# A Winograd-like left half in the second MLP product: seven block products, weight sums made by adding transfers, chunks interleaved

## Chip, cores and metric

One Trainium2 chip, one core. The time is the device time of one execution in microseconds (us). The kernel is a float32 decoder trunk of two layers whose weights (about 480 MB) are read once from device memory.

## The reference

For 256 tokens of width 2048, layer 0 mixes tokens with a Mamba-2 SSD mixer and layer 1 with a dilated sliding-window attention; each layer is followed by a squared-ReLU MLP, and a final RMSNorm closes the trunk. What the change touches is the MLP:

```python
def sq_relu_mlp(h, w1, w2):          # h (256, 2048), w1 (2048, 8192), w2 (8192, 2048)
    a = jax.nn.relu(h @ w1)
    return (a * a) @ w2
...
        x = x + sq_relu_mlp(rms_norm(x, norm_mlp[i]), mlp_w1[i], mlp_w2[i])
    return rms_norm(x, final_norm)
```

## The kernel before, in words

Every large product is made in a split form. A float32 weight block of 128x2048 (1 MB) is fetched from memory into a buffer `raw` (L141). ScalarE (ACT) copies it into `wh`, which rounds it to the type that TensorE (PE) multiplies at full rate (L142), and VectorE (DVE) subtracts to get the rest, `wl` (L143). The left operand is held in the same two parts, and three products stand for one: high by high, high by low, low by high. One such block is called a unit. `unit_plan` lists all units in the order in which PE uses them; `take` hands out the next one and fetches units up to three ahead (`LOOKAHEAD`), with three buffers each of `raw`, `wh` and `wl`.

The MLP goes through the 8192 hidden columns in 8 chunks of 1024. For a chunk, eight w1 units (called U here) make 128 hidden columns each, transposed, in one PSUM bank (`cols_units`, matmuls L169, tile `h`). Each is evacuated on ACT and DVE: the two bank halves are added (L187, L189), ReLU and the token's norm factor are applied (L721), the square is taken (L722) and the result is split into the two parts of `act` (L723, L724). Then eight w2 units (called D) multiply `act` by w2: unit (j, q) is rows 512q to 512q+511 of the chunk by output columns 512j to 512j+511, for both halves of the tokens (`rows_unit`, L203 to L205, tile `d`: 2 x 4 x 3 = 24 matmuls). After both q of a j, `add_residual` adds two banks into the running sum `x_res` (L210). The eight U of the next chunk come before the eight D of this one.

The instructions of an engine are put in order by the scheduler of the framework, from priorities and a timeline that it computes itself; `tc.issue_after` pins an instruction behind another one of the same engine. Loads go out on SP's queue. GpSimd (POOL) makes a few small operations. At the very end (`gained`, and the loop behind `mlp(1, ...)`) the squares of `x_res` are summed, `x_res` is multiplied by the final gain into `xf` (L766), and after the mean is known (L775, L777) `xf` is scaled (L781, L783) and stored.

Of the kernel before, what the change touches and what calls it, by code (L numbers as in the profile page):

```python
# [8 lines left out]
F32 = mybir.dt.float32  # L9
# [5 lines left out]
P = 128  # L15
# [22 lines left out]
FC = 8  # L38
# [25 lines left out]
    return plan  # L64


def mlp_plan(layer):
    plan = [("w1", layer, 0, u) for u in range(8)]
    for c in range(FC):
        if c + 1 < FC:  # L70
            plan += [("w1", layer, c + 1, u) for u in range(8)]
        plan += [("w2", layer, c, j, q) for j in range(4) for q in range(2)]
    return plan


# [1 line left out]
def hybrid_trunk_kernel(ctx: ExitStack, tc: tile.TileContext, a: dict, out: bass.AP):  # L77
# [8 lines left out]
    def mm_bank(name):  # L86
        return psum.tile([P, 512], F32, tag="mm", name=name, bufs=4)
# [19 lines left out]

    warm(2)
    plan = unit_plan()
    ready, load, high = {}, {}, {}  # L110
    cursor = [0, 0]
    latest = [None]

    def source(u):
        kind = u[0]
        if kind == "in":
            return a["w_in"][u[1] * 10 + u[2]], 2048
        if kind == "dt":
            return a["w_dt"], 2048
        if kind == "out":  # L120
            return a["w_out"][u[1] * 4 + u[2]], 2048
        if kind == "qk":
# [7 lines left out]
        return a["w2"][((u[1] * FC + u[2]) * 4 + u[3]) * 2 + u[4]], 2048  # L130

    def fetch(i, ends=(16,)):

        src, n = source(plan[i])
        raw = wts.tile([P, 2048], F32, tag="raw", name=f"raw{i}", bufs=3)
# [42 lines left out]
    def cols_many(us, xs, names, cuts=(12,)):  # L178

        banks = cols_units(us[:2], xs, names[:2], cuts, first=True)  # L180
        yield from banks
        for u, name in zip(us[2:], names[2:]):
            yield cols_units([u], xs, [name])[0]

    def cols_sum(ps, name):
        cross = work.tile([P, S], F32, tag="cross", name=name + "x", bufs=2)
        nc.scalar.activation(cross, ps[:, S:], AF.Copy)  # L187
        tot = work.tile([P, S], F32, tag="tot", name=name + "t", bufs=2)
        nc.vector.tensor_tensor(tot, ps[:, :S], cross, ALU.add)  # L189
        return tot  # L190

    def rows_unit(banks, us, lhs, k0, nk, n, first, last):

        ws = [take(*u) for u in us]
        kn = nk * len(us)
        for m in range(NH):
            t = slice(m * P, (m + 1) * P)
            for i in range(kn):
                wh, wl = ws[i // nk]
                c = slice((i % nk) * n, (i % nk + 1) * n)  # L200
                st, sp = first and i == 0, last and i == kn - 1
# [3 lines left out]
                nc.tensor.matmul(banks[m][:, :n], lo, wh[:, c], start=False, stop=sp)  # L205
# [498 lines left out]


    def mlp(layer, pool, xn, done):
        xs, rs, rb = xn.xs, xn.rs, xn.rb

        def up(c):
            act = pool.tile([P, 8, 2, S], F32R, tag="act", name=f"act{layer}_{c}", bufs=2)  # L710
            us, names = [("w1", layer, c, u) for u in range(8)], [f"h{layer}_{c}_{u}" for u in range(8)]
            if c == 0:
                made = cols_many(us, xs, names)
            else:
                made = (cols_units([u], xs, [name], first=name == names[0])[0]
                        for u, name in zip(us, names))
            for u, ps in enumerate(made):
                name = names[u]
                tot = cols_sum(ps, name)
                r = pool.tile([P, S], F32, tag="r", name=name + "r", bufs=2)  # L720
                nc.vector.scalar_tensor_tensor(r, tot, 0.0, rb, op0=ALU.max, op1=ALU.mult)  # L721
                nc.scalar.activation(r, r, AF.Square)  # L722
                nc.scalar.activation(act[:, u, 0, :], r, AF.Copy)  # L723
                nc.vector.tensor_tensor(act[:, u, 1, :], r, act[:, u, 0, :].bitcast(F32), ALU.subtract)  # L724
            return act

        def down(c, act):
            lhs = lambda k, part, t: act[:, k, part, t]
            for j in range(4):
                banks = [mm_bank(f"d{layer}_{c}_{j}_{m}") for m in range(NH)]  # L730
                us = [("w2", layer, c, j, q) for q in range(2)]
                if c == FC - 1 and j == 3:
                    rows_unit(banks, us, lhs, 0, 4, 512, True, True)
                else:
                    for q in range(2):
                        rows_unit(banks, us[q:q + 1], lhs, 4 * q, 4, 512, q == 0, q == 1)
                add_residual(banks, j)
                if c == FC - 1:
                    done(j)

        cur = up(0)
        for c in range(FC):
            nxt = up(c + 1) if c + 1 < FC else None
            down(c, cur)
            cur = nxt

    n1, n2, n3 = Normed(1), Normed(2), Normed(3)
    with ExitStack() as ctx_ssm:
# [3 lines left out]
    with ExitStack() as ctx_att:  # L752
        attention(n2, n3)
    with tc.tile_pool(name="mlp1", bufs=1) as pool:
        fin = pool.tile([P, D], F32, name="fin")
        nc.scalar.dma_start(fin, a["final_norm"].to_broadcast([P, D]))
        ssq = pool.tile([P, NH, 4], F32, name="fssq")
        mean = pool.tile([P, NH, 28], F32, name="fmean")[:, :, :2]
        xf = pool.tile([P, NH, D], F32, name="xf")

        def gained(j):
            c = slice(j * 512, (j + 1) * 512)
            for m in range(NH):
                nc.scalar.activation(ssq_junk, x_res[:, m, c], AF.Square, accum_out=ssq[:, m, j:j + 1])
                eng = nc.vector if j == 3 else nc.gpsimd
                eng.tensor_tensor(xf[:, m, c], x_res[:, m, c], fin[:, c], ALU.mult)  # L766
# [110 lines left out]
```

## Time and profile before

| | |
|---|---|
| median of 3 runs | 2635.85 us (2635.45 to 2635.88) |
| profiled execution, its own time | 2636.67 us |
| span of the profiled execution | 2634.6 us |
| PE matmul busy | 2620.2 us (99%), 14145 matmuls |
| DVE busy | 1701.5 us (65%) |
| ACT busy | 1344.5 us (51%) |
| POOL busy | 109.7 us (4%) |
| moved by DMA | 489.82 MB, mean 186 GB/s |

The span runs from the first to the last instruction; the execution's own time includes what lies around it. Busy times are merged per engine, so overlapped instructions count once. A matmul's own duration is modelled and overlaps that of its neighbours; the distance between two starts says what it costs.

### The profile page before, as it was taken

To read this page: it belongs to the slowest core of one execution; us is meant where nothing else is said; L and a number is where in the kernel's file an instruction comes from. 1 tells how busy PE (TensorE), PEld (TensorE's weight loads), DVE (VectorE), ACT (ScalarE), POOL (GpSimd) and SP (SyncE) were. 2 spreads that over 40 slices of the span, in tenths; PEclk is the share of its full clock that TensorE was granted. 3 is DMA by queue.
4 is the path that set the end of the run, shared out by engine and by line. 5 is a ranking of instruction groups with operands and counts; after the bars stand their busy time and mean duration, and the time that the engine had idled before them with its cause. 6 is when DMAs were issued, how large, how long until landed. Compare 5 with 4: busy or idle time off the path is not lost.

```text
span 2634.6 us, 34347 instructions
## 1 busy us (share of the span) xinstructions
PE 2620.2 (99%) x14145; PEld 2243.9 (85%) x14145; DVE 1701.5 (65%) x1986; ACT 1344.5 (51%) x1676; POOL 109.7 (4%) x75
## 2 busy tenths in 40 slices
PE   9999999999999999999999999999999999999998
PEld 7888888888888888888888998988888888888887
DVE  7888687786655555555556666676665555555554
ACT  6676455554554444444446656656454444444443
POOL 0121021211000000000000000000000000000001
PEclk9999999999999999999999999999999999999999
DMA  7555555555555555555555454444455555555553
GB/s 282 204 176 192 192 192 178 190 181 187 178 190 192 192 192 192 192 191 188 190 188 181 174 170 163 156 158 157 158 208 192 192 192 192 192 191 192 191 188 133
DMA packets 73036, 489.82 MB, mean 186 GB/s; under 512 B 8112, under 2 KB 8752, under 8 KB 18864
## 3 DMA queue, kind: packets, MB, share of 16 engines
q1 hardware_dynamic: 70272, 477.54, 52.3%
q10 hardware_dynamic: 2608, 10.09, 1.2%
q8 instruction: 111, 1.82, 0.3%
q14 instruction: 45, 0.37, 0.0%
HBM read 485.44 MB, written 2.16 MB: 185 GB/s over the span
## 4 chain that ended last, share of the span: by engine, by line
PE 95%; DVE 2%; ACT 1%; DMA 1%; POOL 1%; issue 1%; SPq 0%; ACTq 0%; POOLq 0%; DVEq 0%
PE h L169 27%; PE qk L169 10%; PE d L203 9%; PE d L204 9%; PE d L205 9%; PE c L169 8%; PE wo L204 2%; PE wo L203 2%; PE wo L205 2%; PE z L204 2%; PE z L205 2%; PE z L203 2%; PE v L203 2%; PE v L204 2%; PE v L205 2%; DVE wl L143 1%
## 5 line engine op out<-in xcount | busy, mean ns | idle before, releaser
L143 DVE TENSOR_TENSOR wl<-raw,wh 128x2048 fp32r<-128x2048 f32 (+4 forms) x470 | 1031.1, 2195 | 805.4 <-ACT wh L142 804.7
L142 ACT ACTIVATE wh<-raw 128x2048 fp32r<-128x2048 f32 (+4 forms) x470 | 863.1, 1838 | 941.1 <-PE d L205 391.7
L169 PE MATMUL h<-xn,wh 128*128 128x512 f32 x2048 | 713.7, 394 | 0.0
L169 PE MATMUL h<-xn,wl 128*128 128x256 f32 x2048 | 571.2, 281 | 0.0
L169 PEld LDWEIGHTS h<-xn,wh 128*128 128x128 f32 x2048 | 384.0, 188 | 87.2
L205 PE MATMUL d<-wh,act 128*128 128x512 f32 x1024 | 398.6, 389 | 0.0
L203 PE MATMUL d<-wh,act 128*128 128x512 f32 x1024 | 398.5, 389 | 0.0
L204 PE MATMUL d<-wl,act 128*128 128x512 f32 x1024 | 398.2, 389 | 0.0
L169 PEld LDWEIGHTS h<-xn,wl 128*128 128x128 f32 x2048 | 383.5, 187 | 2.4 <-DVE wl L143 0.3
L169 PE MATMUL c<-xn,wh 128*128 128x512 f32 x768 | 272.9, 398 | 2.0 <-ACT wh L142 1.8
L169 PE MATMUL qk<-xn,wh 128*128 128x512 f32 x768 | 271.1, 395 | 0.0
L205 PEld LDWEIGHTS d<-wh,act 128*128 128x128 f32 x1024 | 192.2, 188 | 40.1
L203 PEld LDWEIGHTS d<-wh,act 128*128 128x128 f32 x1024 | 192.3, 188 | 39.8
L204 PEld LDWEIGHTS d<-wl,act 128*128 128x128 f32 x1024 | 192.2, 188 | 39.3
L169 PE MATMUL qk<-xn,wl 128*128 128x256 f32 x768 | 216.7, 284 | 0.0
L169 PE MATMUL c<-xn,wl 128*128 128x256 f32 x768 | 215.0, 282 | 0.8 <-DVE wl L143 0.8
L169 PEld LDWEIGHTS c<-xn,wh 128*128 128x128 f32 x768 | 143.9, 188 | 37.0 <-ACT wh L142 3.9
L169 PEld LDWEIGHTS qk<-xn,wh 128*128 128x128 f32 x768 | 144.0, 188 | 30.2
L169 PEld LDWEIGHTS c<-xn,wl 128*128 128x128 f32 x768 | 143.9, 188 | 3.3 <-DVE wl L143 1.1
L169 PEld LDWEIGHTS qk<-xn,wl 128*128 128x128 f32 x768 | 143.7, 188 | 3.2 <-issue 2.7
L210 DVE TENSOR_TENSOR x_res<-d,x_res 128x512 f32<-128x512 f32 x128 | 87.9, 687 | 36.7 <-PE d L205 36.7
L204 PE MATMUL z<-wl,xn 128*128 128x512 f32 x256 | 101.4, 396 | 0.5 <-DVE wl L143 0.5
(336 smaller groups left out, 2976.3 us busy)
## 6 DMA issues: line engine op xcount, KB each, us to landing
raw<-in_w SPq DMA_DIRECT2D x256, 1024.0 KB, 4.9
raw<-in_w_in SPq DMA_DIRECT2D x74, 1024.0 KB, 4.9
raw<-in_w_qk SPq DMA_DIRECT2D x48, 1024.0 KB, 4.9
raw<-in_w_out SPq DMA_DIRECT2D x32, 1024.0 KB, 4.9
raw<-in_w_v SPq DMA_DIRECT2D x32, 768.0 KB, 4.3
ab<-acs_rows ACTq DMA_DIRECT2D x8, 1024.0 KB, 6.1
raw<-in_w_o SPq DMA_DIRECT2D x8, 1024.0 KB, 4.8
raw<-in_w_in SPq DMA_DIRECT2D x6, 512.0 KB, 8.0
```

The costliest lines, as they stand in the source:

```text
L142: high[i] = nc.scalar.activation(wh[:, c], raw[:, c], AF.Copy).ins
L143: nc.vector.tensor_tensor(wl[:, c], raw[:, c], wh[:, c].bitcast(F32), ALU.subtract)
L169: latest[0] = nc.tensor.matmul(ps[:, :n], (wh, wl)[part][:, kt * P:(kt + 1) * P], xs[:, kt, :, :].rearrange("p a t -> p (a t)")[:, :n], st ...
L203: nc.tensor.matmul(banks[m][:, :n], hi, wh[:, c], start=st, stop=False)
L204: nc.tensor.matmul(banks[m][:, :n], hi, wl[:, c], start=False, stop=False)
L205: nc.tensor.matmul(banks[m][:, :n], lo, wh[:, c], start=False, stop=sp)
L210: nc.vector.tensor_tensor(xc, banks[m], xc, ALU.add)
```

## The change

The left half of a chunk's second product (output columns 0 to 1023) is a 2x2 by 2x2 block product: token halves by hidden halves, and hidden halves by output halves. For the first seven chunks of each layer it is now formed from seven block products P1 to P7 instead of eight, with sums of blocks as operands. A product is 12 matmuls for one weight block of 128x2048.

The sums of `act` blocks are formed by DVE from the unsplit squares, which are now kept in one tile `r` of 128x8x256, and are split into two parts each (`combine`). The sums of w2 blocks are formed in the tiles `wa` and `wb`: the first block is loaded from SP's queue, the further ones are added to it in place by transfers issued from GpSimd with an adding operation, each after the split of the sum before it. P4 takes the negated sum, which the split makes with a factor of -1. The seven products share three PSUM banks (`x`: P1, P6, P7, P4 in turn; `w`: P5, P3; `z`: P2), and after each the bank's running sum is added to or subtracted from one block of `x_res` (`put`).

The right half keeps its four D units. All PE work of a chunk, with the eight U of the next chunk, follows the list `CHUNK_ORDER`; the splits of MLP weights are pinned in the order of the plan. The last chunk of each layer stays as it was. In the tail the final gain is multiplied in place into `x_res`, and its load is issued when the last chunk's first column block is done, into the place of `wb`.

```diff
+CHUNK_ORDER = ("U0 U1 P1 U2 P2 U3 U4 P5 D20 D21 P3 U5 U6 P6 U7 D30 P7 D31 P4").split()
+WINOGRAD = {
+    "P1": ("wa", 0, 0, True), "P2": ("raw", 1, 0, True), "P5": ("wa", 0, 1, False),
+    "P3": ("wb", 1, 1, True), "P6": ("wa", 1, 1, False), "P7": ("wb", 0, 1, False),
+    "P4": ("wa", 1, 0, False),
+}
...
         for k0, k1 in zip((0, *ends), ends):
             c = slice(k0 * n // 16, k1 * n // 16)
-            load[i] = nc.sync.dma_start(raw[:, c], src[:, c]).ins
-            high[i] = nc.scalar.activation(wh[:, c], raw[:, c], AF.Copy).ins
-            nc.vector.tensor_tensor(wl[:, c], raw[:, c], wh[:, c].bitcast(F32), ALU.subtract)
+            if begins:
+                load[i] = nc.sync.dma_start(raw[:, c], src[:, c]).ins
+            else:
+                nc.gpsimd.dma_start(raw[:, c], src[:, c], accum_op=ALU.add)
+            with ExitStack() as order:
+                if plan[i][0] in ("w1", "w2"):
+                    order.enter_context(tc.issue_after(high[i - 1]))
+                    order.enter_context(tc.issue_after(low[i - 1]))
+                if product == "P4":
+                    high[i] = nc.scalar.activation(wh[:, c], raw[:, c], AF.Copy, scale=-1.0).ins
+                    low[i] = nc.vector.scalar_tensor_tensor(
+                        wl[:, c], raw[:, c], -1.0, wh[:, c].bitcast(F32),
+                        op0=ALU.mult, op1=ALU.subtract).ins
...
+        def combine(c, r):
+            t1, t2 = slice(0, P), slice(P, S)
+            a11, a12, a21, a22 = r[:, :4, t1], r[:, 4:, t1], r[:, :4, t2], r[:, 4:, t2]
...
+            nc.vector.tensor_tensor(s[0], a21, a22, ALU.subtract)
+            split(1, s[0])
+            nc.vector.scalar_tensor_tensor(s[1], s[0], -1.0, a11, op0=ALU.mult, op1=ALU.subtract)
+            split(2, s[1])
+            nc.vector.scalar_tensor_tensor(s4, a12, -1.0, s[1], op0=ALU.mult, op1=ALU.subtract)
+            split(4, s4)
+            nc.vector.tensor_tensor(s3, a11, a21, ALU.add)
+            split(3, s3)
...
+        def product(c, item, ps, lhs, first):
+            wh, wl = take("w2", layer, c, item)
+            with tc.issue_after(latest[0]):
+                for i in range(4):
+                    n = slice(i * 512, (i + 1) * 512)
+                    for part, w in ((0, wh), (0, wl), (1, wh)):
+                        latest[0] = nc.tensor.matmul(
+                            ps, lhs(i, part), w[:, n], start=(first and i == 0 and part == 0 and w is wh),
+                            stop=(i == 3 and part == 1), skip_group_check=True).ins
+        def put(m, j, ps, op):
+            xc = x_res[:, m, j * 512:(j + 1) * 512]
+            nc.vector.tensor_tensor(xc, xc, ps, op)
...
+                    for m, j, op in {"P1": [(0, 0, ALU.add)], "P2": [(0, 0, ALU.add)],
+                                     "P5": [(1, 1, ALU.add)], "P3": [(0, 1, ALU.subtract)],
+                                     "P6": [(0, 1, ALU.subtract)], "P7": [(1, 1, ALU.add)],
+                                     "P4": [(1, 0, ALU.subtract)]}[item]:
+                        put(m, j, banks[where], op)
...
-        xf = pool.tile([P, NH, D], F32, name="xf")
+        xf = x_res
         def gained(j):
+            if j == 0:
+                fin.append(pool.tile([P, D], F32, tag="wb", name="fin", bufs=1))
+                nc.scalar.dma_start(fin[0], a["final_norm"].to_broadcast([P, D]))
```

## Rows read from the trace of the kernel before

**Rows 1.** The page: span, busy time by engine, the chain by engine.
```profile
span 2634.6 us, 34347 instructions
...
PE 2620.2 (99%) x14145; PEld 2243.9 (85%) x14145; DVE 1701.5 (65%) x1986; ACT 1344.5 (51%) x1676; POOL 109.7 (4%) x75
...
PE 95%; DVE 2%; ACT 1%; DMA 1%; POOL 1%; issue 1%; SPq 0%; ACTq 0%; POOLq 0%; DVEq 0%
```
**Rows 2.** Windows, one MLP chunk: busy us by engine, PEclk, DMA share, GB/s.
```profile
2141.80:2230.00 88.20, 88.20 (x451) 75.16 (x450) 49.95 (x48) 38.61 (x40) 0.00 (x0) 1.00 0.55 191
```
**Rows 3.** The chain in order of time: start us, us, what.
```profile
2141.80 44.65 PE h L169 x256
2230.00 44.65 PE h L169 x256
```
**Rows 4.** Timeline of PE, one w2 unit: start us, us, instruction.
```profile
900.29 0.39 PE L203 MATMUL d<-wh,act 128*128 128x512 f32 x1
...
905.73 0.39 PE L203 MATMUL d<-wh,act 128*128 128x512 f32 x1
```
**Rows 5.** All waits of PE, whole run: us in total, times, longest.
```profile
PE c L169 <- ACT wh L142: 1.8, 2, 1.5
PE warm L106 <- DVE ssq_junk L101: 1.5, 1, 1.5
PE c L169 <- DVE wl L143: 0.8, 1, 0.8
PE yT L557 <- ACT xd L547: 0.7, 1, 0.7
PE z L204 <- DVE wl L143: 0.5, 1, 0.5
PE o L203 <- ACT oT L690: 0.5, 1, 0.5
```
**Rows 6.** Groups by line and shape: busy us, mean ns, idle before, releaser.
```profile
L143 DVE TENSOR_TENSOR wl<-raw,wh 128x2048 fp32r<-128x2048 f32 x419 | 959.9, 2291 | 742.5 <-ACT wh L142 741.8
L142 ACT ACTIVATE wh<-raw 128x2048 fp32r<-128x2048 f32 x419 | 802.3, 1915 | 908.0 <-PE d L205 391.7 <-PE h L169 309.5 <-PE wo L205 81.6
...
L210 DVE TENSOR_TENSOR x_res<-d,x_res 128x512 f32<-128x512 f32 x128 | 87.9, 687 | 36.7 <-PE d L205 36.7
...
L226 ACT ACTIVATE ssq_junk<-x_res 128x512 f32<-128x512 f32 x24 | 15.0, 625 | 9.5 <-DVE x_res L210 7.8 <-DVE xn L221 1.6
...
L414 DVE TENSOR_TENSOR xdds<-xdd,xdds 128x512 fp32r<-128x512 f32 x8 | 5.5, 682 | 0.0
```
**Rows 7.** Timeline of ACT, then DVE, at a chunk's start.
```profile
2230.04 1.92 ACT L142 ACTIVATE wh<-raw 128x2048 fp32r<-128x2048 f32 x1 [3.52 <-PE d L205]
...
2231.99 2.29 DVE L143 TENSOR_TENSOR wl<-raw,wh 128x2048 fp32r<-128x2048 f32 x1 [1.26 <-ACT wh L142]
2237.45 2.29 DVE L143 TENSOR_TENSOR wl<-raw,wh 128x2048 fp32r<-128x2048 f32 x1 [3.16 <-ACT wh L142]
2239.66 0.42 DVE L189 TENSOR_TENSOR h_0t<-h,h_0x 128x256 f32<-128x256 f32 x1
```
**Rows 8.** DMA issues: queue, count, KB each, median us to landing.
```profile
raw<-in_w SPq DMA_DIRECT2D x256, 1024.0 KB, 4.9
...
x_res<-in_x SPq DMA_DIRECT2D x2, 1024.0 KB, 8.0
...
fin<-in_final_norm ACTq DMA_DIRECT2D x1, 1024.0 KB, 6.5
```
**Rows 9.** Timeline of DVE, then ACT, in the tail.
```profile
2626.36 0.69 DVE L210 TENSOR_TENSOR x_res<-d,x_res 128x512 f32<-128x512 f32 x1 [1.68 <-PE d L205]
2627.08 0.69 DVE L766 TENSOR_TENSOR xf<-x_res,fin 128x512 f32<-128x512 f32 x1
2627.90 0.21 DVE L775 TENSOR_SCALAR fmean<-fssq,fmean 128x1 f32<-128x1 f32 x1
...
2627.14 0.63 ACT L764 ACTIVATE ssq_junk<-x_res 128x512 f32<-128x512 f32 x1 [2.01 <-DVE x_res L210]
```

More of the change, by code (lines that the diff above doesn't have):

```diff
@@ L70, in mlp_plan @@
         if c + 1 < FC:
-            plan += [("w1", layer, c + 1, u) for u in range(8)]
-        plan += [("w2", layer, c, j, q) for j in range(4) for q in range(2)]
+            for item in CHUNK_ORDER:
+                if item[0] == "U":
+                    plan.append(("w1", layer, c + 1, int(item[1])))
+                elif item[0] == "P":
+                    plan.append(("w2", layer, c, item))
+                else:
+                    plan.append(("w2", layer, c, int(item[1]), int(item[2])))
+        else:
+            plan += [("w2", layer, c, j, q) for j in range(4) for q in range(2)]
     return plan
@@ L109, in hybrid_trunk_kernel @@
     plan = unit_plan()
-    ready, load, high = {}, {}, {}
+    ready, load, high, low = {}, {}, {}, {}
+    mlp_pool, sums_of = [None], {}
     cursor = [0, 0]
@@ L129, in source @@
             return a["w1"][(u[1] * FC + u[2]) * 8 + u[3]], 2048
-        return a["w2"][((u[1] * FC + u[2]) * 4 + u[3]) * 2 + u[4]], 2048
+        if len(u) == 4:
+            q, j = WINOGRAD[u[3]][1:3]
+        else:
+            j, q = u[3:]
+        return a["w2"][((u[1] * FC + u[2]) * 4 + j) * 2 + q], 2048
     def fetch(i, ends=(16,)):
         src, n = source(plan[i])
-        raw = wts.tile([P, 2048], F32, tag="raw", name=f"raw{i}", bufs=3)
+        product = plan[i][3] if plan[i][0] == "w2" and len(plan[i]) == 4 else None
+        where, _, _, begins = WINOGRAD.get(product, ("raw", 0, 0, True))
+        if where == "raw":
+            raw = wts.tile([P, 2048], F32, tag="raw", name=f"raw{i}", bufs=3)
+        elif begins:
+            raw = sums_of[where] = mlp_pool[0].tile([P, 2048], F32, tag=where, name=f"{where}{i}", bufs=1)
+        else:
+            raw = sums_of[where]
         wh = wts.tile([P, 2048], F32R, tag="wh", name=f"wh{i}", bufs=3)
@@ L140, in fetch @@
             c = slice(k0 * n // 16, k1 * n // 16)
-            load[i] = nc.sync.dma_start(raw[:, c], src[:, c]).ins
-            high[i] = nc.scalar.activation(wh[:, c], raw[:, c], AF.Copy).ins
-            nc.vector.tensor_tensor(wl[:, c], raw[:, c], wh[:, c].bitcast(F32), ALU.subtract)
+            if begins:
+                load[i] = nc.sync.dma_start(raw[:, c], src[:, c]).ins
+            else:
+                nc.gpsimd.dma_start(raw[:, c], src[:, c], accum_op=ALU.add)
[8 more added lines that the diff above has]
+                        op0=ALU.mult, op1=ALU.subtract).ins
+                else:
+                    high[i] = nc.scalar.activation(wh[:, c], raw[:, c], AF.Copy).ins
+                    low[i] = nc.vector.tensor_tensor(wl[:, c], raw[:, c], wh[:, c].bitcast(F32),
+                                                     ALU.subtract).ins
             yield
@@ L204, in rows_unit @@
                 nc.tensor.matmul(banks[m][:, :n], hi, wl[:, c], start=False, stop=False)
-                nc.tensor.matmul(banks[m][:, :n], lo, wh[:, c], start=False, stop=sp)
+                latest[0] = nc.tensor.matmul(banks[m][:, :n], lo, wh[:, c], start=False, stop=sp).ins
     def add_residual(banks, j):
@@ L727, in down @@
[L727 to L745, printed above, removed]
+        mlp_pool[0] = pool
+        def in_order(make):
+            with tc.issue_after(latest[0]):
+                return make()
+        def chunk(c):
+            act = pool.tile([P, 8, 2, S], F32R, tag="act", name=f"act{layer}_{c}", bufs=2)
+            r = pool.tile([P, 8, S], F32, tag="r", name=f"r{layer}_{c}", bufs=1)
+            return act, r
@@ new lines, in put, with half @@
+        def put(m, j, ps, op):
+            xc = x_res[:, m, j * 512:(j + 1) * 512]
+            nc.vector.tensor_tensor(xc, xc, ps, op)
+        act, r = chunk(0)
+        us, names = [("w1", layer, 0, u) for u in range(8)], [f"h{layer}_0_{u}" for u in range(8)]
+        for u, ps in enumerate(cols_many(us, xs, names)):
+            evacuate(0, u, ps, act, r)
+        for c in range(FC - 1):
+            parts = combine(c, r)
+            act_next, r_next = chunk(c + 1)
+            banks = {}
+            def half(k0, t):
+                return lambda i, part: act[:, k0 + i, part, t]
+            t1, t2 = slice(0, P), slice(P, S)
+            of = {"P1": half(0, t1), "P2": half(4, t1), "P4": half(4, t2)}
+            for k, item in ((1, "P5"), (2, "P6"), (3, "P7"), (4, "P3")):
+                of[item] = lambda i, part, k=k: parts[k][:, i, part]
+            lhs = lambda k, part, t: act[:, k, part, t]
+            for item in CHUNK_ORDER:
+                if item[0] == "U":
+                    u = int(item[1])
+                    ps = in_order(lambda: cols_units([("w1", layer, c + 1, u)], xs,
+                                                     [f"h{layer}_{c + 1}_{u}"], first=(u == 0))[0])
+                    evacuate(c + 1, u, ps, act_next, r_next)
+                elif item[0] == "D":
+                    j, q = int(item[1]), int(item[2])
+                    if q == 0:
+                        banks[j] = [mm_bank(f"d{layer}_{c}_{j}_{m}") for m in range(NH)]
+                    in_order(lambda: rows_unit(banks[j], [("w2", layer, c, j, q)], lhs, 4 * q, 4, 512,
+                                               q == 0, q == 1))
+                    if q == 1:
+                        add_residual(banks[j], j)
+                else:
+                    where = {"P1": "x", "P6": "x", "P7": "x", "P4": "x", "P5": "w", "P3": "w",
+                             "P2": "z"}[item]
+                    first = where not in banks
+                    if first:
+                        banks[where] = sm_bank(f"p{where}{layer}_{c}")
+                    product(c, item, banks[where], of[item], first)
+                    for m, j, op in {"P1": [(0, 0, ALU.add)], "P2": [(0, 0, ALU.add)],
[3 more added lines that the diff above has]
+                        put(m, j, banks[where], op)
+            act, r = act_next, r_next
@@ new lines, in mlp @@
+        c = FC - 1
+        lhs = lambda k, part, t: act[:, k, part, t]
+        for j in range(4):
+            banks = [mm_bank(f"d{layer}_{c}_{j}_{m}") for m in range(NH)]
+            us = [("w2", layer, c, j, q) for q in range(2)]
+            if j == 3:
+                rows_unit(banks, us, lhs, 0, 4, 512, True, True)
+            else:
+                for q in range(2):
+                    rows_unit(banks, us[q:q + 1], lhs, 4 * q, 4, 512, q == 0, q == 1)
+            add_residual(banks, j)
+            done(j)
@@ L765, in gained @@
                 eng = nc.vector if j == 3 else nc.gpsimd
-                eng.tensor_tensor(xf[:, m, c], x_res[:, m, c], fin[:, c], ALU.mult)
+                eng.tensor_tensor(xf[:, m, c], x_res[:, m, c], fin[0][:, c], ALU.mult)
             if j == 2:
```

36 lines of the change are left out of this document (19 added, 17 removed).

## The prediction

> **What bounds the kernel now.** I read the page's busy line and chain first. TensorE is busy 2620.2 of 2634.6 us, the chain that ended last is 95% PE, and the other engines stand at 65% (DVE), 51% (ACT) and 4% (POOL) [rows 1]. Then I asked the stage that the change touches: in one steady MLP chunk, from one chunk's first matmul to the next one's, PE is busy 88.20 of 88.20 us, DVE 49.95, ACT 38.61, POOL 0, the DMA engines 0.55, and the granted clock is 1.00, which is 2.4 GHz [rows 2]. The chain in order of time shows what the 88.20 us are: 44.65 us of h matmuls (eight w1 units, 5.58 us each), then 43.55 us of d matmuls (eight w2 units, 5.44 us each) [rows 3]. Two d matmuls 24 apart in the PE timeline start 5.44 us apart, so one 512-column matmul costs 0.2267 us of PE's time; the 0.39 us that the row gives as its duration overlaps its neighbours and must not be used [rows 4]. PE's own waits in the whole run are a few single events of 1.8 us or less, none of them at h or d [rows 5]. So in this stage time is the number of PE columns, and everything else only has to keep up.
>
> **What is removed.** In 7 of 8 chunks of each layer (14 in all) the left half of the second product, four w2 units of 24 matmuls = 96, becomes seven products of 12 = 84. 14 x 12 = 168 matmuls of the same shape go; PE should issue 14145 - 168 = 13977. At 0.2267 us: **-38.1 us**, if the rest still hides. A chunk becomes 8 x 5.58 + 4 x 5.44 + 7 x 2.72 = 85.48 us. The eighth chunk of each layer is unchanged. Bound on the other side: nothing else on PE shortens, since it has no idle time in the stage to give back [rows 2].
>
> **What is added, per chunk.** A unit of a product takes 2.72 us on PE but still a whole 1 MB block and a whole split, so there are 19 fetches and splits for 16.
>
> DVE: 3 more splits at 2.29, 11 instead of 8 additions into x_res (4 for the right half, 7 for the products) at 0.69, and for the left operands 4 sums and 4 low parts of 128x512, priced from another 128x512 two-input row at 0.68 [rows 6]: 6.87 + 2.07 + 5.44 = 14.4 us. DVE goes from 49.95 to 64.3 of 85.48 us, 75%. ACT: 3 splits at 1.92 and 4 copies of 128x512 at 0.63 [rows 6]: 38.61 + 8.3 = 46.9 us, 55%. Neither is the bound, so I cost both at nothing; the cover is PE's work, and it runs out only if a split comes late (second rival). Negated splits and the use of scalar_tensor_tensor for one product are priced as the plain split; the row of that shape is the nearest.
>
> How late a split may be: a split needs its buffer's last user, three units back, to be done on PE, so it has the two units in between. Before that was 10.9 us at least; now a product is next to a U or a D unit everywhere in the order, so it is at least 2.72 + 5.44 = 8.16 us. The chain of one split is ACT 1.92, then DVE 2.29, 4.2 us in all; in the trace high starts at 2230.04, low at 2231.99, and DVE had stood waiting for ACT before that. 4 us are left for the evacuation of a U unit (three DVE pieces of 0.42) and a put (0.69), which is enough [rows 7].
>
> Waits added. (a) P1's load into wa is on SP's queue and waits for P4's split of the chunk before, which runs while P7 and D31 do; it is wanted some 15 us later, and the loads queued behind it have raw buffers that fall free earlier and are wanted later still. Before, SP's loads went out as buffers fell free and landed 4.9 us after issue [rows 8]. Cost 0. (b) P3, P6, P7 and P4 go on in a bank that a put must have read; between a product and the next one in its bank stands a whole D unit at least (5.44 us against 0.69). Cost 0. (c) The single r tile: the next chunk's U0 may be evacuated only when the sums are made; they need U7, which ends 16.3 us before U0 begins, and U0 takes 5.58 more. Cost 0. (d) The adding transfers wait on POOL's queue, where nothing else stands in this stage (POOL busy 0) [rows 2].
>
> **The adding transfers**, 4 a chunk, are an operation that the trace does not show, so they are bounded. A plain 1 MB takes 0.55 x 88.20 / 16 = 3.03 us of all 16 DMA engines [rows 2]. From below: an adding one costs that, 3.03. From above: reading the weights, reading the old sum and writing the new one each as much as a whole plain transfer, 9.1 us. The chunk's traffic is then 15 x 3.03 + 4 x 3.03 = 57.6 us, or 45.5 + 36.4 = 81.9 us, of 85.48. I take the double, 6.1 us (one more read for the same write): 69.8 us, 82%. Latency: for P5, the tightest of the four, its block may be added once P1's split is over, about 4.2 us into U0, and PE wants P5 after U0, U1, P1, U2, P2, U3, U4 = 33.4 us; less 4.2 for the split itself, 25 us are left, against 4.9 us for a plain landing and 8.0 for the slowest 1 MB row (x_res, loaded beside others) [rows 8]. Cost 0 at either end.
>
> The Trainium skill (Collectives: The Full Stack, "The bandwidth ceiling: the fold count and why AG ≠ RS ≠ AR") says that a reducing transfer is slow not for its addition but because it reads two sources, and gives 32.35 GB/s against 62.28 for a copy. By it the adding transfer would be 1.93 x 3.03 = 5.8 us, an estimate, and the sum would stay as it is. No run here shows it yet.
>
> **The tail.** The final gain is now multiplied in place, so the last multiplication must wait for the last Square to have read x_res. Before, both began when x_res was ready (DVE at 2627.08, ACT at 2627.14, to 2627.77), and the mean followed at 2627.90 [rows 9]. Now the multiplication (0.69) comes after the Square, and the mean after it on DVE's queue: +0.7 us; if DVE is given the mean first, 0. I take **+0.7**. The load of the final gain moves from the start of the last MLP to the first column block of its last chunk. It landed in 6.5 us [rows 8]; POOL, which multiplies by it, has the three further blocks of two 5.44 us units each to catch up. Cost 0.
>
> **Sum.** The profiled execution took 2636.67 us, span 2634.6 and 2.1 around it. 2636.67 - 38.1 + 0.7 = 2599.3. The median shown is 0.8 lower, so **2598.5 us**, 1.4% faster.
>
> **Rivals.**
>
> *Second: one split per chunk is late.* Around a chunk's end (U7 D30 P7 D31 P4) the sums and their splits pile on DVE. If the planner puts all eight DVE operations (5.4 us) and the evacuation of U7 (1.3) ahead of one weight split, that split takes 4.2 + 5.4 + 1.3 = 10.9 us in a window of 8.16: PE waits 2.7 us a chunk, 14 x 2.7 = 38 us, all that was won: 2637, no change. For it: DVE and ACT serve their queues in order, and DVE is at 75%. Against: the sums are not wanted before P5, four U units later, the splits have an order of their own, and in the trace small DVE work slots into the gaps in which DVE waits for ACT (1.3 to 3.2 us each) [rows 7]. Half of it, 2618, is likelier than all.
>
> *Third, the slower one: the adding transfers set the pace.* With x us of all 16 engines per adding MB a chunk cannot be shorter than 45.5 + 4x. That passes 85.48 at x = 10.0 (3.3 times a plain transfer) and the old 88.20 at 10.7 (3.5 times); from there the change loses. At 4 times, 12.1, a chunk is 94.0 us: 14 x 8.5 = 119 us, 2718. For it: no such transfer has been timed, and with 0.55 of the DMA engines' time gone already three more blocks a chunk come on top. Against: it needs more than the three full passes of the upper bound.
> The Trainium skill (SBUF — State Buffer, "Who interferes with whom") adds a second way into this rival: GpSimd writes the descriptors of the transfers that it issues, and is shut out while DVE runs in a two-port mode. By it a transfer could start up to one DVE operation late, 2.29 us by the longest row, inside the 25 us of lead; the trace has no GpSimd transfer to hold it against.
>
> **How the numbers follow.** All hidden, 2596 to 2606: 0.60. Part of the second rival, 2606 to 2630: 0.13. All of it, about 2637: 0.07. The third, or a worse pile-up: 0.18. Below 2595, where some PE time would have to vanish that no row shows: 0.02. About 0.2% (5 us) is what a measurement of this kernel can tell from no change. So faster 0.75, same 0.07, slower 0.18. The range 2595 to 2640 takes the first three and leaves 0.2 out; the likeliest case by itself is 2596 to 2606.
>
> **What would show it.** Right: 13977 PE matmuls, chunk starts 85.5 us apart with PE fully busy between them, DVE near 75%, ACT 55%, DMA share near 0.8, adding transfers landing well under 25 us. The second rival shows as PE idle time at a product or the unit after, released by DVE wl, once a chunk at the same place. The third shows as DMA share near 1, and ACT's wh waiting for a DMA instead of for PE. The forecast falls if chunk starts lie further apart than 86 us, whatever the cause.

## The result, and the profile after

The changed kernel takes 2601.14 us (median of four runs, 2599.40 to 2605.23) against 2635.77 us (four runs) for the kernel before beside it: ratio 0.9864, 95% interval 0.9852 to 0.9876. The profiled execution took 2599.40 us; the sum of the prediction for that execution was 2599.3, and for the median 2598.5. Two later executions, one of e10 (3180.19 us) and one of e11 (5211.79 us), fell in a much slower state and are left out of every number below.

The page of the changed kernel answers to [rows 1]: 168 matmuls fewer, PE busy 37.9 us less, and still 95% of the chain.

```profile
span 2597.6 us, 34416 instructions
...
PE 2582.3 (99%) x13977; PEld 2211.8 (85%) x13977; DVE 1878.7 (72%) x2182; ACT 1459.1 (56%) x1774; POOL 160.0 (6%) x131
...
PE 95%; DVE 2%; ACT 1%; DMA 1%; POOL 1%; issue 1%; SPq 0%; ACTq 0%; POOLq 0%; DVEq 0%
```

One steady chunk in windows (busy us by engine, granted clock, DMA share, GB/s), which answers to [rows 2]. PE is busy 85.61 of 85.61 us. DVE is at 62.52 and ACT at 46.79 (64.3 and 46.9 were forecast), the DMA engines at 0.79 (0.82).

```profile
2139.42:2225.03 85.61, 85.61 (x438) 72.90 (x437) 62.52 (x63) 46.79 (x47) 3.45 (x4) 1.00 0.79 233
```

The chain in order of time (start us, us, what), for [rows 3]: chunk starts, here U3 with U4, lie 85.62 us apart. A product takes 2.72 us behind a D unit (px at 2200.08) and 2.75 behind a U unit (px at 2213.95). Such hundredths at every change between U and the rest make up the 0.13 us by which a chunk exceeds the forecast 85.48.

```profile
2139.42 11.17 PE h L215 x64
...
2200.08 2.72 PE px L812 x12
...
2213.95 2.75 PE px L812 x12
...
2225.04 11.17 PE h L215 x64
```

PE's waits in the whole run (us in total, times, longest) are six rows, as in [rows 5]; none is at h, d or a product.

```profile
PE c L215 <- ACT wh L187: 2.3, 2, 1.5
...
PE z L250 <- DVE wl L188: 0.3, 1, 0.3
```

The groups by line and shape, for [rows 6]: the negated split costs what the plain one does, and a low part of a sum is the 128x512 row that priced it.

```profile
L188 DVE TENSOR_TENSOR wl<-wa,wh 128x2048 fp32r<-128x2048 f32 x42 | 95.9, 2284 | 4.7 <-ACT wh L187 4.7
...
L792 DVE TENSOR_TENSOR sp<-s,sp 128x512 fp32r<-128x512 f32 x56 | 38.2, 683 | 0.0
...
L183 DVE SCALAR_TENSOR_TENSOR wl<-wa,wh 128x2048 fp32r<-128x2048 f32 x14 | 32.1, 2292 | 32.0 <-ACT wh L182 32.0
```

Now the operation that the trace of before did not have. The page's queues (packets, MB, share of 16 engines) and issues (count, KB, median us to landing): q0 carries only the 56 adding transfers (42 into wa, 14 into wb), so one takes 0.125 x 2597.6 / 56 = 5.80 us of all 16 engines. A plain MB on q1 takes 0.505 x 2597.6 / 441.4 = 2.97 us (462.86 MB are 441.4 blocks of 1024 KB). That is 1.95 times; it lands in 8.2 us where a plain one takes 4.9 [rows 8].

```profile
q1 hardware_dynamic: 68256, 462.86, 50.5%
q0 software_dynamic: 8064, 58.72, 12.5%
...
raw<-in_w SPq DMA_DIRECT2D x214, 1024.0 KB, 4.9
...
wa<-in_w POOLq DMA_DIRECT2D x42, 1024.0 KB, 8.2
```

The Trainium skill (Collectives: The Full Stack, "The bandwidth ceiling: the fold count and why AG ≠ RS ≠ AR") gives 1.93 as the measured ratio of AllGather, which copies, to ReduceScatter, which adds and so reads two sources, between four ranks. This case's 1.95, for transfers from device memory into a tile, agrees in size; that two reads are its cause is not shown here.

GpSimd's timeline (start us, us, instruction, idle before and its releaser) shows when the sums of the chunk are made. The add at 2208.83 is P5's, the next chunk's; PE wants P5 at 2236.2. Less 4.2 for the split, 23 us of lead, of which 8.2 are used. For P4 (2171.59, wanted at 2200.08) it is 24 us.

```profile
2171.59 0.86 POOL L176 DMA_DIRECT2D wa<-in_w  x1 [12.22 <-DVE wl L188]
2208.83 0.86 POOL L176 DMA_DIRECT2D wa<-in_w  x1 [36.38 <-DVE wl L188]
```

The tail, DVE's timeline, for [rows 9]: from the last addition to the scaling it is 2591.83 - 2588.80 = 3.03 us; before, 2628.78 - 2626.36 = 2.42. So +0.6 us: the multiplication starts behind the Square (`ssq_junk`), as forecast (+0.7).

```profile
2588.80 0.69 DVE L256 TENSOR_TENSOR x_res<-d,x_res 128x512 f32<-128x512 f32 x1 [1.07 <-PE d L251]
2590.35 0.69 DVE L900 TENSOR_TENSOR x_res<-x_res,fin 128x512 f32<-128x512 f32 x1 [0.85 <-ACT ssq_junk L898]
...
2591.83 0.88 DVE L915 TENSOR_SCALAR x_res<-x_res,frs 128x512 f32<-128x512 f32 x2 [0.67 <-POOL frs L911]
```

### The profile page after: what moved, and what is told of

It is laid out like the page before. It is cut to its first block, busy times and chain, and to the rows that moved or that the text cites. A ratio compares the mean times of both kernels' runs of the same rounds, so it can differ in the third digit from the quotient of the medians.

```text
span 2597.6 us, 34416 instructions
## 1 busy us (share of the span) xinstructions
PE 2582.3 (99%) x13977; PEld 2211.8 (85%) x13977; DVE 1878.7 (72%) x2182; ACT 1459.1 (56%) x1774; POOL 160.0 (6%) x131
## 3 DMA queue, kind: packets, MB, share of 16 engines
q1 hardware_dynamic: 68256, 462.86, 50.5%
## 4 chain that ended last, share of the span: by engine, by line
PE 95%; DVE 2%; ACT 1%; DMA 1%; POOL 1%; issue 1%; SPq 0%; ACTq 0%; POOLq 0%; DVEq 0%
PE h L215 28%; PE qk L215 10%; PE c L215 8%; PE px L812 6%; PE d L249 5%; PE d L250 5%; PE d L251 5%; PE pw L812 3%; PE wo L250 2%; PE wo L249 2%; PE wo L251 2%; PE z L250 2%; PE z L251 2%; PE z L249 2%; PE v L249 2%; PE v L251 2%
## 5 line engine op out<-in xcount | busy, mean ns | idle before, releaser
L188 DVE TENSOR_TENSOR wl<-raw,wh 128x2048 fp32r<-128x2048 f32 (+4 forms) x428 | 934.6, 2185 | 578.0 <-ACT wh L187 577.0
L187 ACT ACTIVATE wh<-raw 128x2048 fp32r<-128x2048 f32 (+4 forms) x428 | 782.7, 1831 | 640.8 <-PE h L215 216.5
L251 PE MATMUL d<-wh,act 128*128 128x512 f32 x576 | 224.3, 390 | 0.0
L250 PE MATMUL d<-wl,act 128*128 128x512 f32 x576 | 223.9, 389 | 0.0
L249 PE MATMUL d<-wh,act 128*128 128x512 f32 x576 | 218.7, 390 | 0.0
L251 PEld LDWEIGHTS d<-wh,act 128*128 128x128 f32 x576 | 108.1, 188 | 22.6
L249 PEld LDWEIGHTS d<-wh,act 128*128 128x128 f32 x576 | 108.1, 188 | 22.3
L250 PEld LDWEIGHTS d<-wl,act 128*128 128x128 f32 x576 | 108.1, 188 | 22.0
L778 ACT ACTIVATE r<-r 128x256 f32<-128x256 f32 x128 | 52.2, 410 | 101.7 <-DVE r L777 101.7
```

The source lines that it names most:

```text
L188: low[i] = nc.vector.tensor_tensor(wl[:, c], raw[:, c], wh[:, c].bitcast(F32), ALU.subtract).ins
L251: latest[0] = nc.tensor.matmul(banks[m][:, :n], lo, wh[:, c], start=False, stop=sp).ins
L778: nc.scalar.activation(t, t, AF.Square)
```

## The experiments

All start from the changed kernel. Theory: time is PE's columns, and every added thing is hidden. Against it stood the two rivals, and the question how far the cover reaches.

**e1, the changed kernel again**, no edit.

> The changed kernel once more, unedited, to know its own spread beside the runs of the edits. Four runs so far lie from 2599.4 to 2605.2 us while those of the kernel before lie within 0.5 us. Theory 1 (time is the number of PE matmuls, all the rest hides): runs between 2599 and 2606, the shortest at 2599.4. Theory 2 (the adding transfers cost something in some executions): the same here; it differs in the next kernel.

2599.63 us (2598.90 to 2600.79), the kernel before 2635.99: ratio 0.9862 [0.9847, 0.9877] (in brackets, here and below, the 95% interval). The gain stands, at 36.4 us; e2, e3 and e4 were measured beside it.

**e2, is the adding itself a cost?** The further blocks overwrite instead of being added.

```diff
-                nc.gpsimd.dma_start(raw[:, c], src[:, c], accum_op=ALU.add)
+                nc.gpsimd.dma_start(raw[:, c], src[:, c])
```

> The same transfers on GpSimd's queue, but copying instead of adding (so the sums of weight blocks are left out of the computation). Everything else is the same, instruction by instruction. Theory 1: the shortest run is at 2599.4 +- 0.5, DMA share of a steady chunk falls from 0.79 to about 0.67 (4 x (5.8 - 3.0) = 11.2 us less of 85.6), landing from 8.2 to about 5 us. If the adding itself causes the spread of 6 us between runs, all runs here lie within 1 us. Theory 2 (adding costs time even in the shortest runs): shorter than 2599.4 by more than 1 us.

2599.12 us (2598.45 to 2601.36), 0.5 from e1. One chunk in windows, and the page's queue and landing:

```profile
2141.00:2226.60 85.60, 85.60 (x437) 72.89 (x436) 62.50 (x63) 46.80 (x47) 2.12 (x4) 1.00 0.69 234
```
```profile
q0 software_dynamic: 8064, 58.72, 6.6%
...
wa<-in_w POOLq DMA_DIRECT2D x42, 1024.0 KB, 5.2
```

The DMA share falls from 0.79 to 0.69 and the landing from 8.2 to 5.2 us, and the chunk stays at 85.60. The adding is paid in DMA time and landing time (and 0.86 us of GpSimd for an issue instead of 0.53), and all of that is hidden.

**e4, the order and the tail without the seven products.** Eight D units as before, placed between the U units; no sums, no adding transfers.

```diff
-CHUNK_ORDER = ("U0 U1 P1 U2 P2 U3 U4 P5 D20 D21 P3 U5 U6 P6 U7 D30 P7 D31 P4").split()
+CHUNK_ORDER = ("U0 U1 D00 U2 D01 U3 U4 D10 U5 D11 D20 U6 D21 U7 D30 D31").split()
...
-            parts = combine(c, r)
```

> The interleaved order and the in-place tail, but the left half from eight block products again: sixteen units of U and D in turn, no sums. Theory 1: the number of PE matmuls is that of the kernel before, 14145, so the time is the one before plus the tail, 2635.8 + 0.6 = 2636.4 us, within 2. Rival: the interleaving itself brought part of the 34 to 37 us (by shorter waits or a better rhythm at the changes between U and D): 2620 to 2630.

2638.20 us (median of ten), ratio 1.0010 [1.0000, 1.0019]. Against e1 the seven products win 38.6 us; 168 x 0.2267 = 38.1 was the forecast term. Interleaving and tail cost 2.2 us together, with 0.6 for the tail some 1.6 for the interleaving. The interval allows 0 to 5 us for that sum, so by totals alone it is hardly separable. The chain of e4's own trace separates it: a chunk (from U0 with U1 to the next) is 88.36 us long, 0.16 over the 88.20 of [rows 2] with the same matmuls, and the changed kernel's 85.61 is 2.75 below it, 38.5 us in 14 chunks.

```profile
2053.62 11.16 PE h L215 x64
...
2141.98 11.16 PE h L215 x64
```

**e6, the second rival: more work on DVE and ACT.** The sums and their splits are made twice, so eight more DVE operations and four more ACT copies at the place where the pile was feared.

```diff
+            combine(c, r)
             parts = combine(c, r)
```

> The sums of the left operand and their splits are made twice, the first set is thrown away: 8 more DVE operations of 0.68 and 4 more ACT copies of 0.63 in every chunk, at the place where the second rival of the prediction sees the pile-up. DVE goes from 62.5 to 68 of 85.6 us. Theory 1 (the other engines have slack where it counts): 2599.5 to 2602. Rival (a pile of small DVE work puts a weight split late): up to 14 x 5.4 = 76 us more, 2675, with PE waiting for wl once a chunk.

2601.24 us (2599.60 to 2602.95), ratio 0.9864 [0.9850, 0.9879]. The page has DVE 68.4 us busier and PE as it was:

```profile
PE 2583.3 (99%) x13977; PEld 2212.2 (85%) x13977; DVE 1947.1 (75%) x2294; ACT 1482.4 (57%) x1830; POOL 161.8 (6%) x131
```

PE's waits are six groups at the same tiles. The second rival needed a split to be late by one pile of sums; two piles do not make one late.

**e8, the tail given back.** The last column block is multiplied into tiles of its own, so the multiplication need not wait for the Square.

```diff
+                if j == 3:
+                    dst = pool.tile([P, 512], F32, tag="s", name=f"xf{m}", bufs=2)
+                    last.append(dst)
+                eng.tensor_tensor(dst, x_res[:, m, c], fin[0][:, c], ALU.mult)
```

> The changed kernel, but in the last column block the final gain is multiplied into tiles of their own instead of in place, so this multiplication need not wait for the Square. Theory 1 (the in-place tail costs 0.6 us: from the last addition into x_res to the scaling 3.03 us, 2.42 before): that distance goes back to about 2.4, the time is 0.6 lower, 2599.0 beside 2599.6. Rival: the multiplication is off the path, no change of that distance.

DVE's timeline: 2593.66 - 2591.23 = 2.43 us, the tail of before.

```profile
2591.23 0.69 DVE L256 TENSOR_TENSOR x_res<-d,x_res 128x512 f32<-128x512 f32 x1 [1.66 <-PE d L251]
...
2593.66 0.88 DVE L920 TENSOR_SCALAR x_res<-x_res,frs 128x512 f32<-128x512 f32 x2 [0.67 <-POOL frs L915]
```

In total 2599.08 us (2598.61 to 2601.21), ratio 0.9858 [0.9843, 0.9872]: 0.6 us are won in the trace and drown in the spread of the totals. By the trace it is the better version of the two.

**e3, the third rival: double the adding transfers.**

```diff
-                nc.gpsimd.dma_start(raw[:, c], src[:, c], accum_op=ALU.add)
+                for _ in range(2):
+                    nc.gpsimd.dma_start(raw[:, c], src[:, c], accum_op=ALU.add)
```

> Every adding transfer is issued twice, one after the other (so the sums hold a block too often). That adds 4 x 5.8 = 23.2 us of all 16 DMA engines to a chunk's 67.6 (0.79 of 85.61), 90.8 us in all, more than PE's 85.6. Theory 1 with the ceiling of the prediction (a chunk is not shorter than its DMA time): 85.6 becomes 90.8 or more, 14 x 5.2 = 73 us, about 2674, with ACT's wh waiting for DMAs. Rival: the busy share of the DMA engines holds waiting that parallel transfers fill, it is no ceiling at 1.0: 2600 to 2610, share well above 0.9.

2786.38 us, ratio 1.0562 [1.0533, 1.0591]: far above both expectations, 187 us over e1. A stretch of 480 us in windows shows that the DMA engines were not full (0.87), PE was idle for 44 of 480 us, and the granted clock was 0.95. The waits name one place:

```profile
2120.00:2600.00 480.00, 436.14 (x2151) 368.29 (x2152) 312.02 (x308) 232.25 (x235) 34.43 (x40) 0.95 0.87 246
```
```profile
PE px L813 <- ACT sp L792: 109.7, 12, 13.1
```

All 12 of these waits are P4's. In the profiled execution PE stood idle 130 us longer than in the changed kernel (145.6 of the span against 15.3) and was busy 43 us longer (2625.2 against 2582.3), which is the 173 us of its span: a late P4 also runs slowly, for 4.2 to 5.3 us instead of 2.72. GpSimd's timeline, with one row of DVE's, shows where P4 loses time. The second transfer into wb waits 13.52 us for the landing of the first. P4's first transfer into wa needs P6's split of wa, which ends at 2381.46 (2379.17 and 2.29), and stands behind wb's in the queue until 2383.59, some 2 us. The larger part is its landing: it goes out 0.54 us behind wb's second transfer, and the next one into wa, which waits for it, goes out 15.6 us later:

```profile
2368.66 0.86 POOL L177 DMA_DIRECT2D wb<-in_w  x1 [3.44 <-DVE wl L189]
...
2379.17 2.29 DVE L189 TENSOR_TENSOR wl<-wa,wh 128x2048 fp32r<-128x2048 f32 x1
...
2383.05 0.86 POOL L177 DMA_DIRECT2D wb<-in_w  x1 [13.52 <-DMA wb<-in_w]
2383.59 1.22 POOL L177 DMA_DIRECT2D wa<-in_w  x1
2399.21 0.86 POOL L177 DMA_DIRECT2D wa<-in_w  x1 [14.40 <-DMA wa<-in_w]
```

So P4 waits for landings in series, some of them slow, while the DMA engines as a whole are not full. That makes three things to separate: wb's second transfer in front of P4's in the queue, the chain of sums in wa, and traffic.

**e5, no lead at all.** All U first, then all products, one behind the other.

```diff
+CHUNK_ORDER = ("U0 U1 U2 U3 U4 U5 U6 U7 P1 P2 P5 P3 P6 P7 P4 D20 D21 D30 D31").split()
```

> The same units, but in blocks: U0 to U7, then P1 P2 P5 P3 P6 P7 P4, then the four D. Theory 1 with the chain of adding transfers (a sum can be added to only after its split; one link is the landing of 8.2 us and a split of 4.2): P5, P6 and P4 stand three links behind P1 and have 19 us of product work between them instead of a whole chunk. P1's split ends about 1.4 us before U7 does, so P5 can start 11.2 us after U7, P6 at 23.6, P4 at 36.0 instead of 16.3: 19.7 us a chunk, 14 x 19.7 = 276 us, about 2875. Rival (only the sums of work count, all engines have room on average): 2600 to 2610.

2857.25 us, ratio 1.0830 [1.0812, 1.0848]; 2875 had been worked out from the landings and splits. The chain in order of time shows the sums that follow each other through one tile: a split (ACT, then DVE) and an adding transfer of some 7.9 us, three times over, then P4's own split, a put, and only then P4.

```profile
2313.58 1.92 ACT wh L187
2315.53 2.30 DVE wl L188
...
2318.11 7.92 DMA wa<-in_w
...
2330.65 7.95 DMA wa<-in_w
2338.69 1.92 ACT wh L187
...
2343.22 7.87 DMA wa<-in_w
2351.11 1.92 ACT wh L182
...
2357.55 0.61 DVE x_res L818
2358.29 5.36 PE px L812 x12
```

Same transfers, same matmuls, 258 us between two orders: what hides the adding transfers is where the products stand.

**e7, traffic alone, a miss.** Eight copies of 1 MB in device memory for each chunk, with nothing waiting for them.

```diff
+        if plan[i][0] == "w1" and plan[i][2] > 0:
+            junk = dram.tile([P, 2048], F32, tag="junk", name=f"junk{i}", bufs=8)
+            nc.sync.dma_start(junk, src)
```

> Eight further plain 1 MB copies a chunk, of the w1 blocks into a scratch buffer in device memory that nobody reads, on SP's queue. That is 8 x 3.0 = 24 us more of all 16 DMA engines a chunk, as much as the doubled adding transfers brought (23.2), but no sum waits for them. If the 187 us of the doubled transfers came from the DMA engines being full (67.6 + 23.2 = 90.8 us of DMA in a chunk of 85.6), this costs about the same, 2680 to 2790. If they came from the chain (each sum waits for two landings, and for the other tile's transfers on GpSimd's queue), this costs at most what the engines' time asks for, 14 x 6 = 84 us, 2600 to 2685.

2931.53 us, and nothing on the question: nothing held the copies in their places, and all 112 ran at the kernel's start, where the first weights waited behind them (PE's waits):

```profile
PE dt L218 <- ACT wh L190: 162.2, 1, 162.2
```

**e9, the same traffic in its place.** Each copy is pinned behind the load of its w1 block.

```diff
+                if plan[i][0] == "w1" and plan[i][2] > 0:
+                    junk = dram.tile([P, 2048], F32, tag="junk", name=f"junk{i}", bufs=8)
+                    with tc.issue_after(load[i]):
+                        nc.sync.dma_start(junk, src)
```

> The experiment with further traffic again, now with each scratch copy issued right behind the load of its w1 block, so that eight of them fall into every chunk (before, all 112 ran at the kernel's start, where nothing held them; there 112 copies took some 330 us at a DMA share of 0.99, 2.95 us each). 67.6 + 8 x 2.95 = 91.2 us of all 16 DMA engines a chunk. Theory A (a chunk cannot be shorter than its DMA time): 14 x 5.6 = 78 us more, about 2680, DMA share near 1.0, ACT's wh waiting for DMAs. Theory B (the 187 us of the doubled transfers came from GpSimd's queue, where the second transfer into wb waits for the first one's landing and holds up P4's sum for 14 us a chunk, and DMA time is not yet a limit there): 2600 to 2630.

2599.94 us (2598.98 to 2605.13), ratio 0.9858 [0.9844, 0.9873]: no change. The chunk in windows, and the landing of an adding transfer:

```profile
2139.42:2225.03 85.61, 85.61 (x438) 72.91 (x437) 62.50 (x63) 46.67 (x48) 3.46 (x4) 1.00 0.97 331
```
```profile
wa<-in_w POOLq DMA_DIRECT2D x42, 1024.0 KB, 11.2
```

At a share of 0.97 everything still hides; each adding transfer lands 3 us later, inside its lead. A copy took (59.9% x 2597.3 - 50.5% x 2597.6) / 112 = 2.2 us, less than a plain MB, so this run stops just short of a full load and does not show what happens past it. But a share of 0.87 by itself cannot be what cost e3 its 187 us. The 14 us a chunk that theory B gives to the queue are not in e3's rows either: there the queue holds P4's sum for 2.

**e10, only wa's transfers doubled**, wb's left single: the transfer in front of P4's goes, the longer chain in wa stays.

```diff
+                for _ in range(2 if where == "wa" else 1):
+                    nc.gpsimd.dma_start(raw[:, c], src[:, c], accum_op=ALU.add)
```

> Only the three adding transfers into wa are issued twice (their sums hold a block too often), the one into wb once, so that nothing on GpSimd's queue waits for a landing in front of P4's sum but its own pair. DMA time of a chunk 67.6 + 3 x 5.5 = 84 of 85.6 us. From the end of P6's split to the start of P4 there are 30 us in the changed kernel; two landings of some 10 us and a split of 4.2 make 24. Theory B (the order on GpSimd's queue made the 187 us): hidden, 2600 to 2615. Theory A (DMA time alone, 90.8 us, made them): 3/4 of the doubling still costs much of it, 2650 or more.

2665.67 us, ratio 1.0110 [1.0089, 1.0130]. Some 120 of e3's 187 us are gone with one transfer per chunk, wb's second. The issues and landings of the two traces, as means of the 14 chunks, say by what: P4's first transfer goes out 2.8 us after P6's split in e3 and 0.3 us here, and lands 17.2 us after its issue there and 10.4 us here (one of them in the row below). That is 9.3 us a chunk, of which 2.5 are the place in the queue. 66 us over e9, which ran beside it, remain, and the expectation that next to nothing would remain was wrong. In the chunk shown, P5's first add at 2241.11 to P4's start at 2322.95 is 81.8 us; in the changed kernel 2123.2 (85.6 before 2208.83) to 2200.08 is 76.9: the chain of sums in wa had become some 5 us longer than the PE work beside it. It is not so in every chunk: P4 waits in 7 of the 14, 32.7 us in all, and with one wait of 7.4 at a D unit and 17.5 us more of PE's busy time (2599.8 against 2582.3) that makes up the 59 us of the profiled execution (2658.30).

```profile
PE px L813 <- ACT sp L792: 32.7, 7, 7.1
```
```profile
2293.16 10.81 DMA wa<-in_w
```

The timelines of DVE and PE at P4 also show how a late split spreads. The profile puts P4's wait down to ACT's sp, which P4 does not read. What P4 does need is its own split and that P7's put has read the bank; that put (L819) stands on DVE behind P4's split (L184) and one sum of the next chunk (L795), though P7's last matmul began at 2311.67. So PE starts 1.35 us after the split's end (2321.60):

```profile
2319.31 2.29 DVE L184 SCALAR_TENSOR_TENSOR wl<-wa,wh 128x2048 fp32r<-128x2048 f32 x1 [10.28 <-ACT wh L183]
2321.52 0.68 DVE L795 TENSOR_TENSOR s<-r 128x512 f32<-128x512 f32 x1
2322.12 0.68 DVE L819 TENSOR_TENSOR x_res<-x_res,px 128x512 f32<-128x512 f32 x1
...
2322.95 0.76 PE L813 MATMUL px<-wh,act 128*128 128x512 f32 x1 [5.45 <-ACT sp L792]
```

And the windows show the second price: PE idle for 5.45 us, then P4 at a granted clock of 0.62, a mean between the levels of 1.2 and 2.4 GHz, takes 4.61 us instead of 2.72.

```profile
2317.50:2322.95 5.45, 0.00 (x1) 0.03 (x1) 3.64 (x4) 5.01 (x6) 0.00 (x0) 0.69 0.15 23
2322.95:2327.56 4.61, 4.61 (x14) 3.69 (x15) 4.61 (x6) 2.35 (x2) 0.00 (x0) 0.62 0.69 242
```

**e11 and e12, the chain in wa cut.** P1 reads its block from an ordinary raw buffer, and wa gets a load of its own, so P5's sum no longer waits for P1's split; wa's adding transfers stay doubled. One plain MB more per chunk.

```diff
+        if product == "P1":
+            sums_of[where] = mlp_pool[0].tile([P, 2048], F32, tag=where, name=f"{where}{i}", bufs=1)
+            nc.sync.dma_start(sums_of[where], src)
-        if where == "raw":
+        if where == "raw" or product == "P1":
```

> The kernel with the doubled transfers into wa, with one edit that breaks the ring in which wa goes round: P1 takes its block from a plain raw buffer, and the same block is loaded into wa by a further plain transfer, so that P5's additions may begin when that load has landed and not only when P1's split is over (7.6 us later in the trace of the doubled kernel: P4's split ends at 2141.9, P5's first addition goes out at 2154.5, a load lands in 4.9). DMA time rises by 3 us a chunk. Theory C (wa's own ring, splits and landings one after the other, is longer than PE's 85.6 us by the 4.8 us a chunk that the doubled kernel lost): the ring is shorter by 7.6, the loss goes, 2600 to 2615. Theory A (DMA time): slower than the doubled kernel, 2667 and more.

2637.84 us (median of ten, 2627.16 to 2644.11), ratio 1.0002 [0.9989, 1.0015]: 28 of the 66 us went with the cut, 38 stayed, so neither theory's range held. e12 is the same kernel once more, for its trace:

> The kernel of the run before once more, for its trace: it took 2638 us, between the 2615 of theory C and the 2667 of the doubled kernel. Theory C: P5's first addition goes out some 7 us earlier against PE than in the doubled kernel and PE no longer waits for P5; what is left, 2.8 us a chunk, is a wait at P6 or P4, whose two landings each have got longer (10 to 13 us instead of 8.2) with a DMA share near 0.9. Rival (the ring has nothing to do with it): the waits are spread over units of all kinds, and loads of raw are late.

2631.42 us. A stretch of 500 us in windows, and the wait:

```profile
2050.00:2550.00 500.00, 486.92 (x2470) 412.70 (x2468) 351.54 (x349) 260.66 (x265) 34.57 (x40) 1.00 0.92 272
```
```profile
PE px L816 <- ACT sp L795: 22.1, 8, 5.0
```

All 8 waits are P4's. P5 waits nowhere, but it did not in e10 either, so the cut shows in how long P4 waits (22.1 us in all for 32.7) and not in where. The chain in this stretch runs through transfers that take 10 to 13 us (the page's medians: 10.9 into wa, 7.6 into raw). Waits and slower matmuls (2590.7 busy against 2582.3) make up its 32 us. How much of the remainder is wa's own chain and how much the slower transfers, the raw loads among them, stays open.

## Why the prediction was right

**The main term.** 168 matmuls at the spacing of [rows 4], -38.1 us: measured 38.6 between e4 and e1, 38.5 by the chunks of their traces, and 37.9 in PE's busy time before and after. That a stage with PE at 88.20 of 88.20 [rows 2] is bought and paid for in columns is shown, by e2, e6 and e9 as well: DMA, DVE and ACT work was taken away or added there, and the chunk stayed at 85.6.

**What was missing.** The sum had no term for the interleaving: 0.13 us a chunk in the trace, 1.8 in all. I priced a product at 12 x 0.2267 and a U unit at 5.58 and did not ask what a change between them costs. With tail and interleaving the sum is 2636.67 - 38.1 + 0.6 + 1.8 = 2601.0; the profiled execution took 2599.40, the median 2601.14. That the first sum fell so near its execution is partly luck: 1.6 us went the other way. The traces say where. The first h matmul comes at 694.5 us where it came at 695.2 before, and this start differs from execution to execution (697.0 in e8): 0.7. Around the span lie 1.8 us instead of 2.1: 0.3. The rest, some 0.6, lies where the two MLPs begin: layer 0's first whole chunk took 0.54 us more than a steady one before (88.74 us) and takes 0.12 more now (85.73), and layer 1's first eight U take 47.12 us instead of 47.38.

**The tail** was right in cause and size (+0.6 for +0.7), and e8 takes it away by the cause named.

**Costs taken as nothing.** DVE and ACT came out within 2 us of the forecast per chunk; e6 shows reserve beyond them. The adding transfer, taken at 6.1 us between 3.03 and 9.1, is 5.80.

**The second rival** is refuted by e6. **The third** had the right danger and the wrong deciding point. I put it at the DMA time of a chunk, 45.5 + 4x, deciding from x = 10. By that formula e3 (44.6 + 8 x 5.80 = 91 us a chunk) should have cost 75 us and cost 187, at a share of 0.87; e9, also 91 us by the expected prices, cost nothing at 0.97. What decides first is serial: three sums through the one tile wa, each a landing and a split behind the other (e5, e10), with landings that grow when transfers go out close together (e3: 17.2 us beside wb's for 10.4 without). In the changed kernel that chain has room: three landings of 8.2, four splits of 4.2 and a load of 4.9 are 46 of 85.6 us.

**A wrong "tightest".** P5's lead was worked out as 25 us and is 23; taken alone it is the smallest, by a microsecond. By the forecast's own rule P4's would have been 24.7 (33.1 us of units from U5 to D31, less twice 4.2), and it was not worked out. When transfers get longer, it is P4 that waits and P5 never (e3, e10, e12). The likely reason is that lateness adds up along wa, of which P4 is the last user; e12 shortens the chain and P4's waits with it, but does not remove them.

**The rival from GpSimd's descriptors** did not show. The adding transfers' issues took 867 ns (mean of the 42 into wa) and 862 (14 into wb) with DVE busy for 73% of the chunk, and 0.86 is also what each row of the timeline has. The rule of the Trainium skill (SBUF — State Buffer, "Who interferes with whom") is thus not seen at work here. Nor does it apply as the prediction used it: the same section says that tensor_tensor has no two-port mode, and the 2.29 us row was a TENSOR_TENSOR.

## What to carry to other kernels

Where one engine is busy for all of a stage, price the change in that engine's own spacing, and then ask of every added transfer two things apart from its bandwidth: which chain of waits through one buffer it lengthens, and which other transfer goes out right before it, since both its turn and its landing can come late. A sum made in place by transfers is hidden as long as its whole chain, landings and splits included, is shorter than the stage and its users are spread over it; the order of the users alone was worth 258 us here. A late operand costs more than its wait: the put behind the late split on an in-order engine, and the matmuls that follow at a lower granted clock.

## What the runs showed of the hardware

- An adding transfer of 1 MB from device memory takes 5.80 us of the 16 DMA engines and lands in 8.2 us; a plain one 2.97 and 4.9. Its issue holds GpSimd for 0.86 us, that of a plain one (e2) for 0.53. Issued right behind another adding transfer it landed in 17.2 us on the mean, without that one in 10.4 (e3, e10).
- A DMA share of 0.97 at 331 GB/s cost a kernel with enough lead nothing (e9); landings grew from 8.2 to 11.2 us.
- After 5.45 us without a matmul the granted clock stood at 0.62 for the next product, which took 1.7 times as long (e10).
- Left open: whether the right half could follow the left. 14 x 2.97 + 8 x 5.80 = 88 us of DMA time would stand against about 82.8 us of PE work (an estimate from the rows above; it was not tried). That sum alone does not decide it: e9, at 91 us by the same prices, still kept its chunk of 85.61.
